# Half-tile loads and per-column value storage in a banded-attention kernel, with up-projection operands in one tile per slice

## The chip, the cores and the metric

The kernel runs on one core of a Trainium2 chip. The core has a matrix engine (TensorE, "PE" in the profile, with its weight loads as "PEld"), VectorE (DVE), ScalarE (ACT), GpSimd (POOL), and SyncE (SP), which in this kernel only issues DMAs; 16 DMA engines carry them. The metric is the device time of one launch in microseconds (us); lower is better.

## The reference

One encoder layer is applied to two sequences, one of 512 tokens (s = 0) and one of 2048 (s = 1), with model width 1024, in float32:

```python
x = layer_norm(x, emb_ln_g, emb_ln_b)
z = x @ w_in                                   # 1024 -> 1952, split in eight parts
o_a = natten(qa, ka, va, na_rpb)               # banded attention on a grid of 64 columns, 4 heads of 64
o_b = fourier_mix(fb)
o_c = mla(cq, ckv, kr, ...)                    # full attention, 4 heads
o_d = spatial_gating(sg, ...)
x = layer_norm(ALPHA * x + concat(o_a, o_b, o_c, o_d) @ w_out)
h = conv3(x @ w_up)                            # 1024 -> 2 * 2816, a convolution of width 3 along tokens
x = layer_norm(ALPHA * x + (gelu(h_gate) * h_val) @ w_down)
```

In `natten` a token in grid row r and column c attends to 8 rows by 16 columns around it. The score has a bias from the table `na_rpb`, taken by the difference of rows and of columns.

## The kernel before

Each float32 product is made of three matmuls: an operand is split into a high part (a rounded copy) and a low part (the rest), and hi·hi, hi·lo and lo·hi are added in PSUM. Intermediate results are kept in DRAM between stages, and every load and store is a DMA that SP issues, in one order. A scheduler sets the order of the instructions on each engine when the program is built, from the order in which the code is written and from buffers that come free; inside the stage `far` the PE order is pinned to that of the code.

The stages that the change touches:

- `near` (first part of phase 1): the first layer norm, and the projections for q, k, v, the gating branch and part of the MLA branch, in five blocks of 512 tokens. `feat` makes q and k with features on partitions, `keyed` makes v with tokens on partitions; both split and store hi and lo. q goes to `zq` as three copies (hi, lo, hi), k to `zk` as two (hi, lo), v to `zv`, indexed by token, head pair, and hi or lo.
- `far` (second part of phase 1): the rest of the projections (600 matmuls of 512 columns, five weight groups by five blocks), in between which the generator `natten` runs the banded attention. Its unit of work is one band of rows, one range of 32 key columns (`CW`, four of them), and one head: 80 units in 10 bands, of 384, 512 or 256 keys. While the matmuls of the projection go on (about six between two units), unit x makes its scores, x-2 is transposed, x-4 is multiplied with the values, x-7 is finished.
- Loads of `natten`: `band` fetches, for two heads, q and k with hi on partitions 0 to 63 and lo on 64 to 127, six units ahead; a second copy of q has the halves exchanged, so that two matmuls give the four products. `window` fetches the values for one range of columns, in chunks of four rows by 32 columns. `table` fetches the bias table, three units ahead, from `R`, where eight rows by 16 columns by n keys are read with overlap; POOL then adds the mask, and DVE adds the table to the scores.
- `ffn_up`: three blocks of at most 900 columns (`FF_BLOCKS`). `operands` transposes x2 (the input) in four slices k of the contraction, builds seven Strassen operands from each (B11, T2, T1, T3, B21, T4, B22) and splits them; `features` then multiplies them, for each of 22 pairs of feature tiles f, with seven weight combinations that `weights` makes in the first block and `weights_again` reloads in the others. Between the features of blocks 2 and 3, `down_ops` prepares the operands of the down-projection, two at a time. An operand is one tile for hi and one for lo, over all four slices; x2 is loaded into two buffers (`xs`), which one slice fills.

Of the kernel before, what the change touches and what calls it, by code (L numbers as in the profile page):

```python
# [15 lines left out]
P = 128  # L16
# [22 lines left out]
HW = 450  # L39
# [65 lines left out]
class Builder:  # L105
# [77 lines left out]
    def build(self):  # L183
        tc, nc, I = self.tc, self.nc, self.I
        with tc.tile_pool(name="cst", bufs=1, reuse_waits="tile") as cst, tc.tile_pool(name="scr", bufs=1, space=bass.MemoryType.DRAM) as scr:
# [24 lines left out]
            self.zq = [[d([3, P, T], f"zq{s}_{j}") for j in range(2)] for s, T in SEQS]  # L210
            self.zk = [[d([2, P, T], f"zk{s}_{j}") for j in range(2)] for s, T in SEQS]
            self.zv = [d([T, 2, 2, P], f"zv{s}") for s, T in SEQS]
# [56 lines left out]
    def phase1(self):  # L269
# [6 lines left out]
        def near(wp, sp, pp):  # L276
# [129 lines left out]
            def feat(b, n, uT=None):  # L406
# [281 lines left out]
    def natten(self, wp, pp):  # L688
# [8 lines left out]
        def band(s, j, i):  # L697
# [3 lines left out]
            for hh in range(2):  # L701
                q = self.t(wp, [P, 2, 4, P], "q", F32R, bufs=4)
                for x in range(2):
                    self.load(q[:, x].bitcast(F32).rearrange("p c q -> p (c q)"),
                              self.zq[s][j][x:x + 2, half[hh], i * 512:(i + 1) * 512])
                self.load(kt[:, hh, :n].bitcast(F32), self.zk[s][j][:, half[hh], r0 * GRID_W:r0 * GRID_W + n])
                qk[s, j, i, hh] = q, kt[:, hh]

        def window(s, j, i, c):
# [3 lines left out]
            z = self.zv[s]  # L713
# [440 lines left out]
    def ffn_up(self):  # L1154
# [7 lines left out]
        with tc.tile_pool(name="xo", bufs=1, reuse_waits="tile") as xo, tc.tile_pool(name="fu", bufs=1, reuse_waits="tile") as sp:  # L1162
# [8 lines left out]
            def operand(name, k, hw, src, lo_eng):  # L1171
                self.split(src, X[name, 0][:, k, :hw], X[name, 1][:, k, :hw], "act", lo_eng)

            def operands(bi):
# [26 lines left out]
                for name in names:  # L1201
                    for i in range(2):
                        X[name, i] = self.t(xo, [P, KH, HW], f"{name}{i}", F32R)
                for k in range(KH):
                    xs = [self.t(self.wr2, [P, 8, P], "xs", bufs=2) for _ in range(2)]
                    for h, (_, pieces) in [(h, x) for h in range(2) for x in halves]:
                        i = 0
                        while i < len(pieces):
                            at, n, c, s, row = pieces[i]
                            x2 = self.x2[s].rearrange("t (h k e) -> t h k e", h=2, k=KH)[:, h, k]  # L1210
                            m = 1
                            while n == P and i + m < len(pieces) and pieces[i + m][1] == P and pieces[i + m][3:] == (s, row + m * P):
                                m += 1
                            if m > 1:
                                self.load(xs[h][:, at:at + m], x2[row:row + m * P].rearrange("(t p) e -> p t e", p=P))
                            else:
                                self.load(xs[h][:n, at], x2[row:row + n])
                            i += m
# [27 lines left out]
                return segs, w, hw  # L1246
# [33 lines left out]
            def product(ps, u, name, hw, first, last):  # L1280
                xh, xl = X[name, 0], X[name, 1]
                mm = nc.tensor.matmul
                for k in range(KH):
                    a, b = u[:, k], u[:, KH + k]
                    mm(ps[:, :hw], a, xh[:, k, :hw], start=first and k == 0, stop=False, skip_group_check=True)  # L1285
                    mm(ps[:, :hw], a, xl[:, k, :hw], start=False, stop=False, skip_group_check=True)  # L1286
                    mm(ps[:, :hw], b, xh[:, k, :hw], start=False, stop=last and k == KH - 1, skip_group_check=True)  # L1287
# [45 lines left out]
            meta = {}  # L1333
# [284 lines left out]
```

## Time and profile before

| | |
|---|---|
| median of 3 runs (lowest, highest) | 3687.84 us (3685.08, 3689.01) |
| the profiled execution: its time, its span | 3691.13 us, 3689.3 us |
| PE, DVE, POOL, ACT busy, share of the span | 86%, 57%, 42%, 38% |
| DMA: bytes, mean rate | 673.10 MB, 182 GB/s |

The profile is of one execution of its own; its sums go against 3691.13 us. A view by windows gives, for a stretch of the span, the busy time of each engine, the granted clock of the PE (1.0 is 2.4 GHz, 0.5 is 1.2 GHz), the mean busy share of the 16 DMA engines and the rate in GB/s. "SPq" is SP's issuing; its time for one issue holds what the issue had to wait for in the DMA queue. `near` ends at 368 us, `natten` at about 1077 us, `ffn_up` begins at about 1931 us.

### The profile page before, as it was taken

Reading aid. Unit: us, or ns where it says so; the run is one execution under the profiler, and the core shown is the slowest. Engines: PE = TensorE matmul, PEld = TensorE weight load, DVE = VectorE, ACT = ScalarE, POOL = GpSimd, SP = SyncE. Lnnn points to the kernel's source line nnn. Section 1 sums busy time; section 2 is a strip of 40 time slices with the busy share of each in tenths; the row PEclk is TensorE's granted clock in tenths of the full one; section 3 lists DMA queues with packets and bytes.
Section 4 is the critical chain, followed back from the end, with each engine's and each line's share of the span. In section 5 each row is a group of like instructions: output and inputs, shape, how many; then the busy total and the mean of one; then the engine's idle time right before and its main releaser. Section 6 shows DMA issues by size and latency. Waiting matters only on the chain.

```text
span 3689.3 us, 47183 instructions
## 1 busy us (share of the span) xinstructions
PE 3182.8 (86%) x16423; PEld 2783.3 (75%) x16423; DVE 2106.2 (57%) x3789; ACT 1417.8 (38%) x2566; POOL 1533.9 (42%) x1267
## 2 busy tenths in 40 slices
PE   6999545434569899999998999999999999999997
PEld 5888334334458788887877999899979998787886
DVE  5352112111226788886456887667555655768778
ACT  4232112111235577665224444444334432325223
POOL 7040001001022467654347887555225421546546
PEclk9999767666789999999999999999999999999999
DMA  8564442324354212113447676799758977657653
GB/s 274 184 223 146 138 127 98 120 88 129 104 165 137 78 29 63 33 31 112 153 148 231 237 244 240 250 338 339 238 186 314 335 269 282 212 201 260 216 190 138
DMA packets 417153, 673.10 MB, mean 182 GB/s; under 512 B 51600, under 2 KB 267760, under 8 KB 413844
## 3 DMA queue, kind: packets, MB, share of 16 engines
q1 hardware_dynamic: 416916, 670.09, 53.0%
q8 instruction: 130, 2.13, 0.2%
q14 instruction: 107, 0.88, 0.1%
HBM read 447.02 MB, written 222.97 MB: 182 GB/s over the span
## 4 chain that ended last, share of the span: by engine, by line
PE 68%; DMA 11%; SPq 10%; DVE 5%; ACT 2%; issue 2%; POOL 2%; DVEq 0%; ACTq 0%; POOLq 0%
SPq L126 9%; PE s L120 9%; PE mm L120 7%; PE s L1286 5%; PE s L1287 5%; PE s L1285 5%; PE t L1480 5%; PE t L1285 4%; PE t L1286 4%; PE t L1287 4%; PE t L120 4%; DMA tbl<-R 3%; PE s L1480 3%; PE o L1480 3%; PE t L980 3%; DMA vt<-zv 2%
## 5 line engine op out<-in xcount | busy, mean ns | idle before, releaser
L144 POOL TENSOR_TENSOR w<-wraw,w 128x512 fp32r<-128x512 f32 x162 | 236.5, 1464 | 315.6 <-ACT w L134 266.1
L730 POOL TENSOR_TENSOR tbl<-tbl,mask 128x384 f32<-128x384 f32 (+2 forms) x60 | 63.2, 1056 | 719.8 <-DMA tbl<-R 716.6
L120 PE MATMUL o<-vt,p 128*128 128x128 f32 x512 | 97.2, 324 | 250.2 <-DMA vt<-zv 138.2
L120 PEld LDWEIGHTS o<-vt,p 128*128 128x128 f32 x512 | 86.2, 234 | 274.1 <-DVE on L775 105.2
L1286 PE MATMUL s<-B,w 128*128 128x450 f32 (+1 forms) x792 | 285.8, 361 | 6.9 <-DVE B L144 6.9
L1285 PE MATMUL s<-B,w 128*128 128x450 f32 (+1 forms) x792 | 285.8, 363 | 0.6 <-ACT B L134 0.6
L1287 PE MATMUL s<-B,w 128*128 128x450 f32 (+1 forms) x792 | 285.5, 360 | 0.0
L1285 PE MATMUL t<-T,w 128*128 128x450 f32 (+1 forms) x792 | 282.5, 361 | 2.9 <-DVE u L1166 1.9
L1287 PE MATMUL t<-T,w 128*128 128x450 f32 (+1 forms) x792 | 284.8, 360 | 0.0
L1286 PE MATMUL t<-T,w 128*128 128x450 f32 (+1 forms) x792 | 284.8, 360 | 0.0
L120 PE MATMUL mm<-a,a 128*128 128x512 f32 x600 | 192.4, 468 | 102.9 <-DMA a<-xd 102.9
L744 DVE CUSTOM_DVE_ANT_0 E<-s,tbl,high 128x384 f32<-128x384 f32 (+2 forms) x80 | 51.4, 642 | 371.7 <-POOL tbl L730 348.5
L120 PEld LDWEIGHTS mm<-a,a 128*128 128x128 f32 x600 | 137.7, 235 | 137.1 <-DMA a<-xd 108.3
L120 PE MATMUL s<-a,Q 96*128 96x512 f32 x816 | 223.0, 405 | 7.7 <-POOL Q L138 3.4
L1293 DVE SCALAR_TENSOR_TENSOR h<-h,convc,h 128x896 f32<-128x896 f32 (+1 forms) x132 | 218.8, 1690 | 0.0
L952 DVE TENSOR_SCALAR_CACHE_REDUCE a<-s,low 128x512 f32<-128x512 f32 x272 | 195.4, 745 | 32.2 <-PE t L980 23.9
L1480 PE MATMUL t<-w,go 128*128 128x512 f32 x696 | 194.6, 399 | 3.8 <-ACT go L134 2.0
L1292 DVE SCALAR_TENSOR_TENSOR h<-h,convc,h 128x896 f32<-128x896 f32 (+1 forms) x132 | 164.6, 1277 | 53.8 <-ACT h L1291 53.8
L1291 ACT ACTIVATE h<-h,convc 128x896 f32<-128x896 f32 (+1 forms) x132 | 138.3, 1095 | 136.3 <-DVE h L1166 135.3
L747 ACT ACTIVATE E<-E,nam 128x384 f32<-128x384 f32 (+2 forms) x80 | 51.0, 637 | 347.3 <-DVE nam L744 347.2
L144 DVE TENSOR_TENSOR a<-t,a 128x512 fp32r<-128x512 f32 x240 | 161.1, 683 | 33.7 <-ACT a L134 32.8
L134 ACT CAST w<-wraw 128x512 fp32r<-128x512 f32 x166 | 102.0, 618 | 188.4 <-PE t L1287 137.9
(326 smaller groups left out, 9039.0 us busy)
## 6 DMA issues: line engine op xcount, KB each, us to landing
w<-wuops SPq DMA_DIRECT2D x220, 512.0 KB
wuops<-w SPq DMA_DIRECT2D x110, 512.0 KB
w<-wdops SPq DMA_DIRECT2D x104, 512.0 KB
wraw<-in_w_up_dram SPq DMA_DIRECT2D x88, 512.0 KB
wdops<-xs SPq DMA_DIRECT2D x74, 512.0 KB
graw<-g SPq DMA_DIRECT2D x100, 256.0 KB
wd<-wdops SPq DMA_DIRECT2D x48, 512.0 KB
a<-xd SPq DMA_DIRECT2D x20, 1024.0 KB
```

Of the source, the lines that this page charges most:

```text
L120: return self.pe(self.nc.tensor.matmul(*a, **k))
L126: self.nc.sync.dma_start(out, in_)
L144: e.tensor_tensor(lo, src, hi.bitcast(F32), op=ALU.subtract)
L952: nc.vector.tensor_scalar(e[:, c * 512:c * 512 + 512], ps, 1.0, self.low, op0=ALU.mult, op1=ALU.max, accum_out=m4[:, c:c + 1])
L980: nc.tensor.transpose(pt[:, k], e[:, kk * P:(kk + 1) * P], self.ident)
L1285: mm(ps[:, :hw], a, xh[:, k, :hw], start=first and k == 0, stop=False, skip_group_check=True)
L1286: mm(ps[:, :hw], a, xl[:, k, :hw], start=False, stop=False, skip_group_check=True)
L1287: mm(ps[:, :hw], b, xh[:, k, :hw], start=False, stop=last and k == KH - 1, skip_group_check=True)
L1291: nc.scalar.activation(c[:, :n], hb[:, 0:n], AF.Identity, bias=cb[:, ft:ft + 1], scale=cw[:, 0, ft:ft + 1])
L1292: nc.vector.scalar_tensor_tensor(c[:, :n], hb[:, 1:n + 1], cw[:, 1, ft:ft + 1], c[:, :n], op0=ALU.mult, op1=ALU.add)
L1293: nc.vector.scalar_tensor_tensor(c[:, :n], hb[:, 2:n + 2], cw[:, 2, ft:ft + 1], c[:, :n], op0=ALU.mult, op1=ALU.add)
L1480: mm = lambda a, b, st, sp_: nc.tensor.matmul(ps, a, b, start=st, stop=sp_, skip_group_check=True)
```

## The change

Four edits:

- `band`: q and k come in one transfer per half (hi or lo) of 64 partitions, in place of one per tile of 128 partitions; so 8 transfers of q and 4 of k per band, before 4 and 2. `zq` has two copies, hi and lo, and no third.
- `keyed` and `window`: the values are kept in four DRAM tensors, one per range of 32 columns, where a chunk of four rows is 128 consecutive rows; a column that lies in two ranges is stored twice. One store of 256 tokens is now 16 of 32 tokens; the loads stay 128, of 128 KB each.
- `ffn_up`: an operand is a tile per slice, with hi and lo in it. The rows of x2 are loaded in a function of their own (`rows_of`), into `xs` for even and `wraw2` for odd slices, two slices ahead; for the next block this begins before the last features of the block. The first weights of a block are made or loaded before its operands.
- `down_ops` is advanced by two and three in turn, and not at the last f of a block.

```diff
-            self.zq = [[d([3, P, T], f"zq{s}_{j}") for j in range(2)] for s, T in SEQS]
+            self.zq = [[d([2, P, T], f"zq{s}_{j}") for j in range(2)] for s, T in SEQS]
-            self.zv = [d([T, 2, 2, P], f"zv{s}") for s, T in SEQS]
+            self.zv = [[d([T // 2, 2, 2 * P], f"zv{s}_{c}") for c in range(4)] for s, T in SEQS]
...
-                for i, a in enumerate((hi, lo, hi) if n[0] == "q" else (hi, lo)):
+                for i, a in enumerate((hi, lo)):
...
-                    r0 = t0 + 2 * t2 * P
-                    self.store(self.zv[s][r0:r0 + 2 * P].rearrange("(t p) j a d -> p t (j a d)", p=P),
-                               z.bitcast(F32).rearrange("p t j a d -> p t (j a d)"))
+                    zz = z.bitcast(F32).rearrange("p t j a d -> p t j (a d)")
+                    for t in range(2):
+                        r0 = (t0 + (2 * t2 + t) * P) // 2
+                        for c in range(4):
+                            for r in range(2):
+                                self.store(self.zv[s][c][r0 + 32 * r:r0 + 32 * r + 32], zz[64 * r + CW[c]:64 * r + CW[c] + 32, t])
...
-                for x in range(2):
-                    self.load(q[:, x].bitcast(F32).rearrange("p c q -> p (c q)"),
-                              self.zq[s][j][x:x + 2, half[hh], i * 512:(i + 1) * 512])
-                self.load(kt[:, hh, :n].bitcast(F32), self.zk[s][j][:, half[hh], r0 * GRID_W:r0 * GRID_W + n])
+                for a in range(2):
+                    for x in range(2):
+                        self.load(q[half[a], x].bitcast(F32).rearrange("p c q -> p (c q)"),
+                                  self.zq[s][j][a ^ x, half[hh], i * 512:(i + 1) * 512])
+                    self.load(kt[half[a], hh, :n].bitcast(F32), self.zk[s][j][a, half[hh], r0 * GRID_W:r0 * GRID_W + n])
...
-                self.load(v[:, k].bitcast(F32), bass.AP(z.tensor, z.offset + ((r0 + 4 * k) * GRID_W + CW[c]) * 512 + j * 256,
-                                                        [[GRID_W * 512, 4], [512, 32], [1, 256]]))
+                self.load(v[:, k].bitcast(F32), self.zv[s][c][(r0 + 4 * k) * 32:(r0 + 4 * k + 4) * 32, j])
...
-                    for i in range(2):
-                        X[name, i] = self.t(xo, [P, KH, HW], f"{name}{i}", F32R)
+                        X[name, k] = self.t(xo, [P, 2, HW], f"{name}{k}", F32R)
...
-                    xs = [self.t(self.wr2, [P, 8, P], "xs", bufs=2) for _ in range(2)]
+                tiles = [self.t(self.wr2, [P, 8, P], ("xs", "wraw2")[k % 2], bufs=2) for _ in range(2)]
...
+            prefetch(0)
+            rows_of(0, 0)
             for bi in range(len(FF_BLOCKS)):
-                meta[bi] = operands(bi)
+                ahead = weights_again(0) if bi else weights(0)
+                if bi == 0:
+                    rows_of(0, 1)
+                operands(bi)
+                last = bi == len(FF_BLOCKS) - 1
                 for f in range(NF):
-                    W = weights_again(f) if bi else weights(f)
-                    if bi:
-                        next(down_ops, None)
-                        next(down_ops, None)
-                    if bi == len(FF_BLOCKS) - 1 and f == NF - 1:
-                        self.down_head()
+                    W = ahead if f == 0 else weights_again(f) if bi else weights(f)
+                    if bi and f < NF - 1:
+                        for _ in range(3 if f % 2 else 2):
+                            next(down_ops, None)
+                    if f == NF - 1:
+                        if last:
+                            self.down_head()
+                        else:
+                            prefetch(bi + 1)
+                            rows_of(bi + 1, 0)
+                            rows_of(bi + 1, 1)
                     features(bi, f, W)
```

SP's queue where `near` gives way to `far`, before: the last stores of k and v, then the first band's q, its mask, tables and values (numbers behind names are those of buffers).

```order
L129 DMA zk_1_26_99<-zs_3252 128x512
L129 DMA zv_28_101<-uv_3306 128x2x512
L129 DMA zv_28_101<-uv_3359 128x2x512
L126 DMA q_3384<-zq_0_21_94 128x1x512 x2
L126 DMA q_3388<-zq_0_21_94 128x1x512 x2
L126 DMA mask_3392<-in_na_mask_dram 128x3x384
L126 DMA tbl_3394<-R_116 128x1x384
```

The same place in the changed kernel, from the second half of the last stores of v on.

```order
L129 DMA zv_0_31_104<-uv_3490 32x512 x2
L129 DMA zv_1_32_105<-uv_3490 32x512 x2
L129 DMA zv_2_33_106<-uv_3490 32x512 x2
L129 DMA zv_3_34_107<-uv_3490 32x512 x2
L126 DMA q_3530<-zq_0_21_94 64x512 x4
L126 DMA q_3537<-zq_0_21_94 64x512 x4
L126 DMA mask_3544<-in_na_mask_dram 128x3x384
L126 DMA tbl_3546<-R_122 128x1x384
```

The two stores of v have become 32 (half of them stand here in part), and the four loads of q eight; the order of mask, tables and values behind them is as it was.

The PE at the change from block 1 to block 2 of `ffn_up`, before (lines L1226 are transposes of x2 for the new block; operands B and T whose last number is below 19000 are still the old block's).

```order
L1226 MATMUL t_19642<-ident_60,xs_19612 128x128 x3
L1226 MATMUL t_19642<-ident_60,xs_19612 128x66
L1285 MATMUL s_19873<-B_4034_19597,w_19845 128x450
L1286 MATMUL s_19873<-B_4035_19598,w_19845 128x450
L1287 MATMUL s_19873<-B_4034_19597,w_19845 128x450
L1226 MATMUL o_19683<-ident_60,xs_19669 128x128 x3
L1226 MATMUL o_19683<-ident_60,xs_19669 128x66
L1226 MATMUL t_19649<-ident_60,xs_19612 128x128 x3
L1226 MATMUL t_19649<-ident_60,xs_19612 128x64
L1285 MATMUL t_19502<-T_3480_16097,w_19479 128x450
```

The same place in the changed kernel.

```order
L1238 MATMUL t_19883<-ident_60,xs_19708 128x128 x3
L1238 MATMUL t_19883<-ident_60,xs_19708 128x66
L1298 MATMUL s_20107<-B_4066_19855,w_19839 128x450
L1299 MATMUL s_20107<-B_4066_19855,w_19839 128x450
L1300 MATMUL s_20107<-B_4066_19855,w_19839 128x450
L1238 MATMUL o_19931<-ident_60,wraw_4046_19717 128x128 x3
L1238 MATMUL o_19931<-ident_60,wraw_4046_19717 128x66
L1238 MATMUL t_19890<-ident_60,xs_19708 128x128 x3
L1238 MATMUL t_19890<-ident_60,xs_19708 128x64
L1298 MATMUL t_19742<-T_3498_16356,w_19699 128x450
```

The sequence is almost the same; the second slice's transposes now read another buffer (`wraw`) than the first slice's.

## Rows read from the trace of the kernel before

**Rows 1.** The page, busy tenths of the PE in 40 slices.
```profile
PE   6999545434569899999998999999999999999997
```

**Rows 2.** Windows: stretch, length, five engines' busy us, PE clock, DMA share, GB/s.
```profile
184.00:368.00 184.00, 183.30 (x1184) 163.70 (x1182) 69.97 (x191) 49.20 (x89) 41.93 (x16) 1.00 0.52 184
368.00:1080.00 712.00, 341.00 (x1532) 279.60 (x1532) 132.40 (x409) 139.21 (x388) 63.20 (x60) 0.70 0.36 117
485.00:500.00 15.00, 0.00 (x0) 0.00 (x0) 0.00 (x0) 0.00 (x0) 0.00 (x0) 0.64 0.13 52
1029.00:1031.00 2.00, 0.06 (x1) 0.09 (x1) 0.56 (x3) 0.03 (x1) 0.72 (x1) 0.50 0.27 92
406.00:408.00 2.00, 0.16 (x1) 0.00 (x0) 0.00 (x0) 0.00 (x0) 0.00 (x0) 0.50 0.47 167
1222.00:1228.00 6.00, 4.46 (x30) 4.32 (x30) 3.41 (x4) 3.31 (x5) 0.00 (x0) 1.00 0.45 142
2400.00:2700.00 300.00, 300.00 (x1462) 275.39 (x1461) 193.66 (x189) 114.67 (x159) 131.44 (x83) 1.00 0.85 297
```

**Rows 3.** Waits, 368 to 1080 us: who waited for whom, us in total, times, longest.
```profile
POOL tbl L730 <- DMA tbl<-R: 716.6, 47, 138.5
```

**Rows 4.** DMA issues of the whole span: out<-in, how many, KB of one.
```profile
vt<-zv SPq DMA_DIRECT2D x128, 128.0 KB
...
q<-zq SPq DMA_DIRECT2D x40, 256.0 KB
...
tbl<-R SPq DMA_DIRECT2D x24, 256.0 KB
...
tbl<-R SPq DMA_DIRECT2D x24, 192.0 KB
...
a<-zk SPq DMA_DIRECT2D x8, 512.0 KB
...
a<-zk SPq DMA_DIRECT2D x8, 384.0 KB
...
a<-zk SPq DMA_DIRECT2D x4, 256.0 KB
```

**Rows 5.** SP's issues by tile: ns of one, least/median/most, first and last start.
```profile
L126 SPq DMA_DIRECT2D q<-zq x40: 509/2652/10237, 381.8 to 1005.4; - x40
...
L129 SPq DMA_DIRECT2D zk<-zs x20: 319/380/1387, 51.9 to 379.6; - x20
...
L126 SPq DMA_DIRECT2D raw<-K x20: 444/450/499, 1222.1 to 1681.2; - x20
```

**Rows 6.** Timeline of the PE (start, us, instruction): scores of successive units.
```profile
421.21 0.60 PE L120 MATMUL s<-a,q 128*128 128x384 f32 x2
421.66 1.55 PE L120 MATMUL mm<-a,a 128*128 128x512 f32 x6
...
423.93 0.60 PE L120 MATMUL s<-a,q 128*128 128x384 f32 x2
...
560.22 0.72 PE L120 MATMUL s<-a,q 128*128 128x512 f32 x2
...
563.51 0.72 PE L120 MATMUL s<-a,q 128*128 128x512 f32 x2
...
992.49 0.49 PE L120 MATMUL s<-a,q 128*128 128x256 f32 x2
...
994.88 0.50 PE L120 MATMUL s<-a,q 128*128 128x256 f32 x2
```

**Rows 7.** Windows where the blocks of `ffn_up` begin.
```profile
1925.00:1965.00 40.00, 24.28 (x117) 18.45 (x116) 30.29 (x58) 19.08 (x37) 28.27 (x21) 0.79 0.73 234
2340.00:2370.00 30.00, 24.68 (x106) 19.14 (x105) 21.37 (x46) 17.40 (x32) 17.70 (x16) 0.83 0.53 161
2740.00:2780.00 40.00, 28.27 (x110) 22.02 (x109) 19.61 (x45) 16.61 (x33) 16.20 (x16) 0.66 0.40 124
```

**Rows 8.** What ended the PE's idle time before the transposes of x2 (us, times).
```profile
DMA xs<-x: 26.0, 16
```

More of the change, by code (lines that the diff above doesn't have):

```diff
@@ L712, in window @@
             v = self.t(wp, [P, 4, 2 * P], "vt", F32R, bufs=4)
-            z = self.zv[s]
             for k in range(nch):
-                self.load(v[:, k].bitcast(F32), bass.AP(z.tensor, z.offset + ((r0 + 4 * k) * GRID_W + CW[c]) * 512 + j * 256,
-                                                        [[GRID_W * 512, 4], [512, 32], [1, 256]]))
+                self.load(v[:, k].bitcast(F32), self.zv[s][c][(r0 + 4 * k) * 32:(r0 + 4 * k + 4) * 32, j])
             V[s, j, i, c] = v
@@ L1171, in operand, with prefetch @@
             def operand(name, k, hw, src, lo_eng):
-                self.split(src, X[name, 0][:, k, :hw], X[name, 1][:, k, :hw], "act", lo_eng)
-            def operands(bi):
+                x = X[name, k]
+                self.split(src, x[:, 0, :hw], x[:, 1, :hw], "act", lo_eng)
+            def prefetch(bi):
                 segs = FF_BLOCKS[bi]
@@ L1200, in operands @@
                     halves.append((zeros, pieces))
-                for name in names:
-                    for i in range(2):
-                        X[name, i] = self.t(xo, [P, KH, HW], f"{name}{i}", F32R)
-                for k in range(KH):
-                    xs = [self.t(self.wr2, [P, 8, P], "xs", bufs=2) for _ in range(2)]
[L1206 to L1218, printed above, removed]
+                staged[bi] = halves, hw, []
@@ new lines, in prefetch, with rows_of @@
+                meta[bi] = segs, w, hw
+            def rows_of(bi, k):
+                halves, hw, xs = staged[bi]
+                tiles = [self.t(self.wr2, [P, 8, P], ("xs", "wraw2")[k % 2], bufs=2) for _ in range(2)]
+                xs.append(tiles)
+                for h, (_, pieces) in [(h, x) for h in range(2) for x in halves]:
+                    i = 0
+                    while i < len(pieces):
+                        at, n, c, s, row = pieces[i]
+                        x2 = self.x2[s].rearrange("t (h k e) -> t h k e", h=2, k=KH)[:, h, k]
+                        m = 1
+                        while n == P and i + m < len(pieces) and pieces[i + m][1] == P and pieces[i + m][3:] == (s, row + m * P):
+                            m += 1
+                        if m > 1:
+                            self.load(tiles[h][:, at:at + m], x2[row:row + m * P].rearrange("(t p) e -> p t e", p=P))
+                        else:
+                            self.load(tiles[h][:n, at], x2[row:row + n])
+                        i += m
@@ L1220, in quarter, with operands @@
+            def operands(bi):
+                halves, hw, staging = staged[bi]
+                for k in range(KH):
+                    xs = staging[k]
+                    for name in names:
+                        X[name, k] = self.t(xo, [P, 2, HW], f"{name}{k}", F32R)
                     def quarter(h, i, tag):
@@ L1245, in operands @@
                     operand("B22", k, hw, b22, "dve")
-                return segs, w, hw
+                    if k + 2 < KH:
+                        rows_of(bi, k + 2)
             def weights(f):
@@ L1280, in product @@
             def product(ps, u, name, hw, first, last):
-                xh, xl = X[name, 0], X[name, 1]
                 mm = nc.tensor.matmul
                 for k in range(KH):
+                    xh, xl = X[name, k][:, 0, :hw], X[name, k][:, 1, :hw]
                     a, b = u[:, k], u[:, KH + k]
-                    mm(ps[:, :hw], a, xh[:, k, :hw], start=first and k == 0, stop=False, skip_group_check=True)
-                    mm(ps[:, :hw], a, xl[:, k, :hw], start=False, stop=False, skip_group_check=True)
-                    mm(ps[:, :hw], b, xh[:, k, :hw], start=False, stop=last and k == KH - 1, skip_group_check=True)
+                    mm(ps[:, :hw], a, xh, start=first and k == 0, stop=False, skip_group_check=True)
+                    mm(ps[:, :hw], a, xl, start=False, stop=False, skip_group_check=True)
+                    mm(ps[:, :hw], b, xh, start=False, stop=last and k == KH - 1, skip_group_check=True)
             def conv(hb, ft, n):
@@ L1331, in features @@
                     col += m + 2
-            meta = {}
+            meta, staged = {}, {}
             down_ops = self.down_ops()
+            prefetch(0)
+            rows_of(0, 0)
             for bi in range(len(FF_BLOCKS)):
-                meta[bi] = operands(bi)
-                for f in range(NF):
-                    W = weights_again(f) if bi else weights(f)
-                    if bi:
-                        next(down_ops, None)
-                        next(down_ops, None)
-                    if bi == len(FF_BLOCKS) - 1 and f == NF - 1:
-                        self.down_head()
+                ahead = weights_again(0) if bi else weights(0)
[3 more added lines that the diff above has]
+                last = bi == len(FF_BLOCKS) - 1
+                for f in range(NF):
+                    W = ahead if f == 0 else weights_again(f) if bi else weights(f)
[5 more added lines that the diff above has]
+                            self.down_head()
+                        else:
+                            prefetch(bi + 1)
+                            rows_of(bi + 1, 0)
+                            rows_of(bi + 1, 1)
                     features(bi, f, W)
```

## The prediction

> **What bounds the kernel now.** I read the PE's slices first. They are full almost everywhere but for one stretch: from slice 5 to slice 12 they stand at 3 to 6 tenths [rows 1]. The windows cut it out: in `far`, 368 to 1080 us, the PE is busy 341 of 712 us, at a mean granted clock of 0.70 [rows 2]. So 371 us are idle there, and part of the rest runs at half speed. The waits say for what: POOL waits 716.6 us for the bias tables [rows 3]. That looks like a matter of the tables, but the DMA engines are busy only 0.36 of the time at 117 GB/s [rows 2], and the same kernel holds 297 GB/s elsewhere (2400 to 2700 us). A queue that is late although its engines are mostly idle has its load on few of them. The window 485 to 500 us shows which transfers do that: SP issues loads of q and k there, no engine computes, and the DMA share is 0.13, which is 2 engines of 16, at 52 GB/s. Where values alone come, it is 0.27 (4 engines) at 92 GB/s; where tables do, 0.47 (8 engines) at 167 GB/s [rows 2].
>
> If these groups lie within each other, the two engines that q and k use must also do their part of all else. The stage moves 117 GB/s x 712 us = 83.3 MB. Of that q is 40 x 256 KB and k 8 x 512, 8 x 384 and 4 x 256 KB, together 18.9 MB; the values are 128 x 128 KB = 16.8 MB; the two larger kinds of table make 11.0 MB [rows 4]; some 36.6 MB are left. At the rates seen: 18.9 / 52 = 363 us, 16.8 / 92 = 182 us, 11.0 / 167 = 66 us, and the rest on 16 engines of 26 GB/s (half of 52), 416 GB/s, 88 us. That is 699 us of 712. So I hold that two DMA engines bound the whole stage, and that the tables are only what waits behind them in the queue.
>
> **What the change does to that stage.** Each q or k transfer becomes two of 64 partitions, with one row per partition on both sides; a value chunk becomes 128 rows on both sides. The nearest row for such a transfer is the load of K in the MLA branch, 64 rows like these: SP issues it in 0.45 us [rows 5], and where four of them and their companions run, the share is 0.45 at 142 GB/s [rows 2]. That is far above 0.13 and 52, with SP's own pace as the likely limit. I take all 16 engines. Then bands take 18.9 / 416 = 45 us, values 40 us, tables 66 us as before, the rest 88 us: 239 us. From the other side, 0.36 x 712 = 256 us is what each engine would do if everything were spread evenly; the tables still use half of the engines, 11.0 MB / 26 GB/s = 423 engine-us or 26 us more there than the mean: 282 us. I take 282, the larger.
>
> In the Trainium skill, "DMA: Bandwidth & Descriptors", section "Why a DMA increments its semaphore by 16 and not by 1", the number of engines of a transfer is the largest up to 16 that divides the size of the outermost dimension on both sides. By it q and k (2 halves) get 2, values (4 rows) 4, tables (8 rows) 8, and the changed loads 16. The trace agrees with 0.13, 0.27 and 0.47; the sum by this rule is the one above.
>
> The PE's floor: units follow each other without a gap in 2.72 us (384 keys), 3.29 us (512) and 2.39 us (256), six projection matmuls included [rows 6]. There are 32, 32 and 16 of them (four, four and two bands of eight): 87 + 105 + 38 = 230 us. The 600 - 480 matmuls outside cost 1.55 / 6 = 0.26 us each [rows 6], 31 us: 261 us at full clock. So PE and DMA come out close to each other, and neither will run free. The highest mean DMA share that a long stretch of this trace holds is 0.85 [rows 2], with the PE full beside it; 282 / 0.85 = 332 us. At the start, 30 more stores of v stand ahead of the first q at about 0.4 us each [rows 5], half of them issued before the last matmuls of `near` end, and the last eight units drain without cover: 20 us for both. Stage: 352 us after 712, **-360 us**. Bounds: 292 us (282 and 10 of drain) and 493 us (the second rival), so -420 to -219.
>
> **The smaller terms.** SP issues 60 more transfers for the bands (60 x 0.45 = 27 us of a queue that now has some 370 to issue in 350 us, below 0.6 us each): hidden by the look-ahead of three to six units, and part of the 0.85. In `near` there are 160 stores of v in place of 10 and 10 fewer of q: 140 x 0.38 to 0.45 us [rows 5] = 53 to 63 us of SP in 368 us, and 2.6 MB more. The PE is busy 183.3 of 184 us in the second half of it [rows 2], since its operands are on the chip; the loads that stand behind these stores are the next block's x, wanted a block later. I take +5 us; 0 if all is covered, 15 if every block start is held by one batch of 32 (12 us) once.
>
> `ffn_up`: in the three stretches where blocks begin, 110 us, the PE does 24.28 x 0.79 + 24.68 x 0.83 + 28.27 x 0.66 = 58 us of work at full clock [rows 7]; 52 us are lost. Of that 26.0 us are the PE waiting for the rows of x2 [rows 8], because `xs` holds one slice. With two slices ahead this wait can go. What is late next is the building of operands, four slices on DVE, ACT and POOL: DVE is busy 30.29 of the first 40 us [rows 7]. The tile per slice by itself gives little: a slice's old operand is free less than one product earlier (12 of the 84 matmuls of an f, some 2.4 us), and the PE's order at the boundary is nearly as before. I take -20 us; 0 if operands simply become the wait, -40 if the clock stays up too, and a loss of up to 10 if buffers shared with the weights hold something up. `down_ops` at 2.5 per f for 30 f in place of 2 for 37: an operation moves 0.67 MB (a store of 512 KB, and a seventh of two loads of as much), and an f lasts 17 us (1462 matmuls in 300 us, 84 per f), so half an operation more is 19 GB/s on 297 [rows 2]: share 0.90, no cost; up to 10 us if the weights come late in the f with three.
>
> **Sum.** 3691.1 (the profiled execution) - 360 - 20 + 5 = 3316 us; the median of the shown runs lies 3.3 us below the profiled one: **3313 us**.
>
> **Rivals.**
> 1. Look-ahead and clock take much of it back. For it: tables are fetched three units ahead, some 9 us, and a band's burst (2 MB and a mask, and projection operands of 1 MB each) goes through the same queues; one issue of q took up to 10.2 us [rows 5]; after each gap the PE runs at half clock. If the mean clock stays at 0.70, the PE alone needs 261 / 0.70 = 373 us, and a wait of 10 us in each of ten bands gives 473; with the 20 us, 493 us. Total 3691 - 219 - 15 = 3457. Against it: bursts shorten most of all.
> 2. The stage runs on its floor, 292 us, and the block starts give 30: 3691 - 420 - 30 = 3241. For it: where no transfer is late, units already follow each other without a gap [rows 6]; against: DMA and PE would both have to be over 0.9 busy.
> 3. Slower: the halves bring nothing, because two transfers to 64 partitions take as long together as the one took, and SP only has more to issue. It decides if a half runs at 52 GB/s or less. Then the stage stays at 712 us, plus 60 x 0.45 = 27 us, plus 12 us of stores ahead of the first band: 3691 + 39 = 3730. Against it: 142 GB/s for K's 64 rows [rows 2].
>
> The skill's same page, in "Rules for kernel authors", advises against two transfers to disjoint partition halves, since both use all engines already. By that rule the third rival holds; the window with 0.13 says that here the one transfer does not use all engines.
>
> **Chances.** The forecast 0.66 (its own range 3250 to 3390), rival 1 0.18, rival 2 0.11, rival 3 0.05. The range 3220 to 3455 holds the forecast, nearly all of rival 2 and half of rival 1. What this measurement can tell from no change is about 0.2%, 7 us. All but rival 3 are faster: 0.95; its 0.05 I split into 0.04 slower and 0.01 within, where losses and small gains would cancel.
>
> **What would show it.** In the changed profile: no stretch with a share of 0.13 in `far`; the first score within 20 us of the end of `near`; the stage's DMA share near 0.75, its clock above 0.9; POOL's wait for tables below 300 us, since POOL, not a bound, always waits for the next one; the PE's gaps before transposes of x2 without the rows' DMA. The forecast is wrong if q still comes at 52 GB/s, if the stage is over 450 us, or if the tables, still on eight engines, have become what all units wait for.

## The result, and the profile after

The changed kernel takes 3313.2 us (median of 3 runs, 3308.36 to 3321.07), the kernel before 3687.84: ratio 0.8988, 95% interval 0.8959 to 0.9017. The prediction was 3313 us. The profiled execution took 3308.36 us (span 3306.6), 382.7 us of span less than that of before.

The PE by slices, and its granted clock, after. The stretch of 3 to 6 tenths [rows 1] is gone; slices 5 to 9 (counted from 1, as there) stand at 8, and the clock there at 8 to 9 tenths.

```profile
PE   6799888889899999999999999999899999999997
...
PEclk9899998989899999999999999999899999999999
```

Windows after: the second half of `near`, `far` from end to end, and three parts of it (columns as in [rows 2]).

```profile
193.00:377.00 184.00, 182.52 (x1180) 162.96 (x1179) 71.41 (x196) 51.13 (x93) 41.92 (x16) 1.00 0.64 210
...
376.80:708.30 331.50, 275.79 (x1520) 235.38 (x1519) 127.66 (x401) 136.71 (x383) 63.50 (x60) 0.90 0.83 240
...
400.00:500.00 100.00, 85.75 (x484) 73.79 (x485) 43.66 (x129) 45.35 (x119) 25.32 (x22) 0.91 0.86 254
500.00:600.00 100.00, 85.08 (x481) 73.23 (x480) 42.55 (x129) 44.60 (x123) 20.84 (x18) 0.90 0.91 251
600.00:700.00 100.00, 82.39 (x454) 70.27 (x452) 36.88 (x132) 41.36 (x127) 17.34 (x20) 0.90 0.84 247
```

The bytes are nearly those of before (331.5 us x 240 GB/s = 80 MB, before 83), and the busy time is near that of before: 0.83 x 331.5 = 275 us of each DMA engine, before 0.36 x 712 = 256. What changed is that all 16 share it; only the tables are still read by eight. The PE's idle time in the stage fell from 371 to 56 us. Its waits in `far`, first before, then after (engine, line, what it waited for: us, times, longest):

```profile
PE o L120 <- DMA vt<-zv: 138.2, 45, 30.6
PE mm L120 <- DMA a<-xd: 102.9, 11, 41.1
PE o L120 <- DVE on L775: 95.0, 14, 32.0
```

```profile
PE o L120 <- DVE on L777: 20.5, 9, 4.7
PE mm L120 <- DMA a<-xd: 12.6, 5, 5.5
PE s L120 <- DMA q<-zq: 7.7, 2, 7.4
PE t L123 <- ACT E L749: 7.5, 3, 5.4
PE o L120 <- DMA vt<-zv: 7.2, 4, 5.6
```

The operands `xd` of the projection have the same 16-engine shape before and after; no edit touches them. They cost 103 us before and 12.6 after; with q and k alone back on two engines (the first experiment below) it is 85.8 us again. So they were late because of what stood ahead of them in the queue. To cut the span into stages, the first and last starts of three groups on the PE, before:

```profile
L120 PE MATMUL mm<-wtok,xTl x320: 279/290/443, 50.8 to 367.8; 128*128 128x256 f32 x80, 128*128 128x288 f32 x80
L120 PE MATMUL o<-vt,p x512: 219/277/477, 423.0 to 1077.0; 128*128 128x128 f32 x171
L1226 PE MATMUL o<-ident,xs x96: 217/273/476, 1931.0 to 2771.5; 128*128 128x128 f32 x68, 64*128 64x64 f32 x8, 1*128 1x1 f32 x8, 65*128 65x65 f32 x4
```

and after:

```profile
L120 PE MATMUL mm<-wtok,xTl x320: 277/290/446, 52.4 to 376.5; 128*128 128x256 f32 x80, 128*128 128x288 f32 x80
L120 PE MATMUL o<-vt,p x512: 220/276/475, 411.2 to 708.0; 128*128 128x128 f32 x171
L1238 PE MATMUL o<-ident,xs x48: 217/272/478, 1563.0 to 2384.2; 128*128 128x128 f32 x34, 64*128 64x64 f32 x4, 1*128 1x1 f32 x4, 65*128 65x65 f32 x2
```

With the start of the last up-projection matmul (3104.7 and 2722.2 us) this gives the ledger:

| part | before, us | after, us | change | predicted |
|---|---|---|---|---|
| to the end of `near` | 367.8 | 376.5 | +8.7 | +5 |
| `far`, to the last value matmul | 709.2 | 331.5 | -377.7 | -360 |
| from there to `ffn_up` | 854.0 | 855.0 | +1.0 | 0 |
| `ffn_up` | 1173.7 | 1159.2 | -14.5 | -20 |
| the rest | 584.6 | 584.4 | -0.2 | 0 |

SP's issues after (ns of one, least/median/most, first and last start); q before was 2652 in the median and up to 10237 [rows 5]:

```profile
L126 SPq DMA_DIRECT2D q<-zq x80: 444/587/1087, 388.7 to 663.6; - x80
```

So it was the backlog of the queue, not the issuing, that took 2.7 us. The median alone is no safe sign of such a queue: with q and k back on two engines it is only 655 ns, and the backlog shows in the longest issue.

```profile
L126 SPq DMA_DIRECT2D q<-zq x40: 493/655/9776, 407.8 to 913.7; - x40
```

### The profile page after: what moved, and what is told of

Its sections match the earlier page's. It is cut to its first block, busy times and chain, and to the rows that moved or that the text cites. A ratio compares the mean times of both kernels' runs of the same rounds, so it can differ in the third digit from the quotient of the medians.

```text
span 3306.6 us, 47401 instructions
## 1 busy us (share of the span) xinstructions
PE 3118.1 (94%) x16423; PEld 2737.1 (83%) x16423; DVE 2112.2 (64%) x3789; ACT 1417.7 (43%) x2566; POOL 1537.0 (46%) x1267
## 4 chain that ended last, share of the span: by engine, by line
PE 41%; DVE 4%; DMA 2%; issue 1%; POOL 1%; ACT 1%; SPq 0%; DVEq 0%; POOLq 0%; ACTq 0%
PE s L1299 6%; PE s L1298 6%; PE s L1300 6%; PE t L1504 5%; PE t L1298 4%; PE t L1299 4%; PE t L1300 4%; PE s L1504 3%; PE o L1504 3%; DMA graw<-g 1%; DVE x L1371 1%; DVE go L144 1%; POOL w L144 1%; DMA wraw<-x 0%; DVE x L1487 0%
## 5 line engine op out<-in xcount | busy, mean ns | idle before, releaser
L732 POOL TENSOR_TENSOR tbl<-tbl,mask 128x384 f32<-128x384 f32 (+2 forms) x60 | 63.5, 1060 | 344.8 <-DMA tbl<-R 332.0
L1306 DVE SCALAR_TENSOR_TENSOR h<-h,convc,h 128x896 f32<-128x896 f32 (+1 forms) x132 | 219.6, 1694 | 0.0
L1305 DVE SCALAR_TENSOR_TENSOR h<-h,convc,h 128x896 f32<-128x896 f32 (+1 forms) x132 | 171.5, 1330 | 53.4 <-ACT h L1304 53.4
L120 PE MATMUL mm<-a,a 128*128 128x512 f32 x600 | 167.8, 422 | 12.6 <-DMA a<-xd 12.6
L120 PEld LDWEIGHTS s<-a,Q 96*128 96x128 f32 x816 | 145.2, 192 | 33.4 <-DVE a L954 4.5
L134 ACT CAST a<-t 128x512 fp32r<-128x512 f32 x240 | 134.1, 585 | 79.2 <-PE t L982 76.5
L982 PE MATMUL t<-ident,a 128*128 128x128 f32 x1088 | 156.2, 275 | 9.6 <-DVE a L144 5.5
L1504 PEld LDWEIGHTS t<-w,go 128*128 128x128 f32 x696 | 130.5, 188 | 40.0 <-ACT go L134 4.4
L134 ACT CAST go<-gs 128x256 fp32r<-128x256 f32 x200 | 78.0, 405 | 195.4 <-PE t L1504 64.7
```

What stands on the lines that cost most here:

```text
L120: return self.pe(self.nc.tensor.matmul(*a, **k))
L134: nc.scalar.copy(out, src)
L982: nc.tensor.transpose(pt[:, k], e[:, kk * P:(kk + 1) * P], self.ident)
L1305: nc.vector.scalar_tensor_tensor(c[:, :n], hb[:, 1:n + 1], cw[:, 1, ft:ft + 1], c[:, :n], op0=ALU.mult, op1=ALU.add)
L1306: nc.vector.scalar_tensor_tensor(c[:, :n], hb[:, 2:n + 2], cw[:, 2, ft:ft + 1], c[:, :n], op0=ALU.mult, op1=ALU.add)
L1504: mm = lambda a, b, st, sp_: nc.tensor.matmul(ps, a, b, start=st, stop=sp_, skip_group_check=True)
```

## The experiments

Times are medians; the kernel before, run beside each of them, took 3687.6 to 3689.7 us, so they can be read against 3313.2 directly.

**Bands undone.** Ratio to before 0.9674 (0.9659 to 0.9688), 3567.8 us.

```diff
-                for a in range(2):
-                    for x in range(2): self.load(q[half[a], x]..., self.zq[s][j][a ^ x, half[hh], ...])
-                    self.load(kt[half[a], hh, :n]..., self.zk[s][j][a, half[hh], ...])
+                for x in range(2): self.load(q[:, x]..., self.zq[s][j][x:x + 2, half[hh], ...])
+                self.load(kt[:, hh, :n]..., self.zk[s][j][:, half[hh], ...])
```

> The changed kernel with the loads of q and k (and the three copies of q) as in the kernel before; values, operands and tables stay changed. Theory A (how many of the 16 DMA engines carry a transfer is set by its outermost dimension, and the fullest engines bound the stage): two engines carry q and k again, 18.9 MB at 52 GB/s = 363 us, and their part of values 40, tables 66 and the rest 88: 557 us for a stage that now takes 331.5 us. far 560 to 600 us, DMA share there near 0.45, whole time 3540 to 3580 us. Theory B (the gain comes from the values' layout, or from look-ahead that any relief gives back): less than 60 us lost, below 3370 us.

`far` of this kernel as a window:

```profile
376.50:974.00 597.50, 304.24 (x1520) 256.10 (x1520) 132.78 (x408) 142.74 (x386) 63.28 (x60) 0.73 0.44 141
```

597.5 us, at a share of 0.44. The sum for two engines, 557 us, is 0.93 of it; in the kernel before it was 699 of 712. The values' layout alone, with q and k on two engines, brings the other 112 us of the stage, no more.

**Values undone.** Ratio 0.9280 (0.9268 to 0.9293), 3422.5 us.

```diff
-                self.load(v[:, k]..., self.zv[s][c][(r0 + 4 * k) * 32:(r0 + 4 * k + 4) * 32, j])
+                self.load(v[:, k]..., bass.AP(z.tensor, ..., [[GRID_W * 512, 4], [512, 32], [1, 256]]))   # and one store per 256 tokens
```

> The changed kernel with the values stored and loaded as before; q and k still come as halves. Theory A: the four engines that values use carry 45 (q, k) + 182 (values) + 66 (tables) + 88 (rest) = 381 us; far 390 to 440 us in place of 331.5, and near gives back its 8.7 us, since 10 stores of v stand there again in place of 160: whole time 3360 to 3410 us. Theory B (values were hidden behind q and k and bound nothing): far within 15 us of 331.5, whole time 3290 to 3315 us. If near does not come back to 368 us, its 8.7 us were not the stores of v.

```profile
370.20:817.60 447.40, 317.32 (x1519) 261.29 (x1519) 126.99 (x401) 134.48 (x383) 63.29 (x60) 0.81 0.58 175
```

The direction of theory A, but 12 us beyond its range: four engines' 381 us make 447, 0.85 and not 0.93 or more of the stage. The last matmul of `near` starts at 369.9 us, so 6.6 of its 8.7 us were the stores of v; in the kernel with `ffn_up` changed alone it starts at 370.1 with the old stores, so the other 2 us are scatter. From both runs: the bands are worth 255 us, the values 109, each with the other already mended.

**`ffn_up` undone, and `ffn_up` alone.** Two kernels: the changed one with the old `ffn_up` (3325.3 us, ratio 0.9017, 0.9004 to 0.9029), and the one before with the new one (3676.7 us, ratio 0.9967, 0.9954 to 0.9979).

```diff
-                        X[name, k] = self.t(xo, [P, 2, HW], f"{name}{k}", F32R)   # and rows_of, first weights, down_ops
+                    for i in range(2): X[name, i] = self.t(xo, [P, KH, HW], f"{name}{i}", F32R)
```

> The changed kernel with ffn_up, its operands and the pace of down_ops as before: the attention part alone. If the two parts add up, the whole time is 14.6 us above that of the changed kernel, by the markers in the two traces: ratio to the kernel before 0.902 to 0.904, near 3327 us. Rival: the 14.6 us are what the slices of x2 wait for in a queue that the attention left late, so that ffn_up is quick by itself: then no loss, ratio 0.898 to 0.900.

> The kernel before with the edit of ffn_up alone (tile per slice, rows of x2 loaded ahead, first weights ahead of the operands, down_ops at 2.5). If it adds up: 14.6 us less, 3673 us, ratio 0.996, the PE's wait for the rows of x2 going from 26.0 us to 22 or less. Rival: no difference within 0.2%.

12 us each way: the parts add up, and `ffn_up` doesn't depend on what the attention does to the queue. In the second kernel the PE's own wait for the rows falls from 19.0 to 8.8 us.

**Rows not ahead.** 3328.4 us, ratio 0.9021 (0.9008 to 0.9035).

```diff
-                tiles = [self.t(self.wr2, [P, 8, P], ("xs", "wraw2")[k % 2], bufs=2) for _ in range(2)]
+                tiles = [self.t(self.wr2, [P, 8, P], "xs", bufs=2) for _ in range(2)]   # rows_of(bi, k) inside the loop over k
```

> The changed kernel with the rows of x2 loaded into the two xs buffers alone, one slice at a time inside the loop over slices, as before; the tile per slice, the first weights ahead of the operands and the pace of down_ops stay changed. If the rows' early loading is what makes ffn_up shorter (the prediction's step), all of its 14.6 us are lost: about 3325 us. If the tile per slice or the weights' earlier place do it, less than 5 us are lost, since the PE still waited 22.1 us for rows in the changed kernel: 3310 to 3318 us.

All of the gain is lost (15 us), so the early rows make it. The PE's waits over the block starts, changed kernel:

```profile
PE t L1238 <- DMA wraw<-x: 7.1, 7, 2.5
...
PE t L1238 <- DMA xs<-x: 2.7, 1, 2.7
...
PE o L1238 <- DMA wraw<-x: 0.6, 1, 0.6
```

and without the early rows:

```profile
PE t L1239 <- DMA xs<-x: 16.0, 6, 5.8
PE s L1298 <- DVE B L144: 7.0, 2, 6.4
PE o L1239 <- DMA xs<-x: 3.2, 5, 1.6
```

10.4 us for the rows against 19.2; and the 7.0 us for the operand B, which is built from them, go with it. `ffn_up` takes 1174.1 us in this run, as long as before the change (1173.7). So the tile per slice, the first weights ahead and the new pace of `down_ops`, which all stayed in, bring nothing that shows; none of them was taken out by itself. The second theory rested on a misreading: the 22.1 us that it named count the PE and its weight loads together, whose waits overlap.

**Stores of v merged.** 3305.3 us, ratio 0.8961 (0.8947 to 0.8974).

```diff
-                                self.store(self.zv[s][c][r0 + 32 * r:r0 + 32 * r + 32], zz[64 * r + CW[c]:64 * r + CW[c] + 32, t])
+                            self.store(dst[r], zz[64 * r + CW[c]:64 * r + CW[c] + 32])   # both t: dst "(t r p) j e -> r p t j e"
```

> The changed kernel with the 16 stores of 32 tokens per 256 tokens of v made 8 of 2 x 32 (the same bytes, 80 issues in place of 160 in near). If the end of near was late (376.8 us for 368.1 before, and the first score 16 us later) because SP issues so many stores, half of both goes: 4 to 10 us less, 3300 to 3309 us. Rival: the bytes, not the issues, hold up the loads: no change within 0.15%, 3308 to 3318 us.

SP where `near` gives way to `far`, changed kernel (start, us, what, how many):

```profile
372.54 16.01 SPq L129 DMA_DIRECT2D zv<-uv  x32
388.65 4.93 SPq L126 DMA_DIRECT2D q<-zq  x8
```

with merged stores:

```profile
365.83 9.29 SPq L129 DMA_DIRECT2D zv<-uv  x16
375.22 5.15 SPq L126 DMA_DIRECT2D q<-zq  x8
```

The same bytes in half the issues: the last matmul of `near` starts at 369.8 us, 6.7 us earlier, and the first q is issued 13.4 us earlier. `far` stays about as long (333.4 us in this run); the medians differ by 8.

**Tables over 16 engines.** 3295.6 us, ratio 0.8928 (0.8912 to 0.8943).

```diff
-            self.load(t[:, :n], bass.AP(self.R.tensor, self.R.offset + a0, [[32, 8], [1, 16], [1, n]]))
+            self.load(t[:, :n], bass.AP(self.R.tensor, self.R.offset + a0, [[1, 16], [32, 8], [1, n]]))   # q, mask, result in that order
```

> The changed kernel with the 128 queries of a unit in another order (16 columns outermost, 8 rows inside), so that a table is read as 16 x 8 x n in place of 8 x 16 x n; q is stored, the mask built and the result put back in that order. Bytes, issues and instructions are the same. Theory A (outermost dimension sets the engines, fullest engine bounds far): the tables spread over 16 engines, the fullest one has 256 us in place of 282, far 331.5 to about 305, whole time 3280 to 3295 us. Rival C (the PE with its half-speed stretches and the queue's order now bound the stage): far within 6 us, whole time 3305 to 3320 us.

```profile
378.80:690.10 311.30, 268.80 (x1519) 231.46 (x1519) 127.90 (x401) 140.38 (x383) 63.29 (x60) 0.92 0.91 255
```

20 us of `far`, where 26 was the price of the unevenness: theory A, at a slightly smaller size (the whole time is 0.6 us above its range).

**One transfer per tile, 128 rows.** 3269.3 us, ratio 0.8855 (0.8837 to 0.8873).

```diff
-            self.zq = [[d([2, P, T], f"zq{s}_{j}") for j in range(2)] for s, T in SEQS]
+            self.zq = [[d([2, 3 * 64, T], f"zq{s}_{j}") for j in range(2)] for s, T in SEQS]   # per head: hi, lo, hi
...
+                for x in range(2): self.load(q[:, x]..., self.zq[s][j][hh, 64 * x:64 * x + P, ...])
```

> The changed kernel, but q and k lie in DRAM per head with the halves behind each other, so that one transfer fills 128 partitions from 128 rows: 2 + 1 transfers per head of a band as in the kernel before (60 fewer issues in far), yet 128 rows outermost; q has its third copy again, and near stores q and k in 64-row pieces (60 more stores). Theory A (the outermost dimension matters, not the halving): far within 15 us of 331.5, whole time 3295 to 3325 us. Theory B (two smaller transfers side by side are what brings the gain): far falls back towards the 597 us that it took with whole tiles of outermost dimension 2, whole time above 3400 us.

```profile
372.80:666.30 293.50, 261.55 (x1519) 226.85 (x1519) 127.66 (x401) 141.21 (x383) 63.67 (x60) 0.94 0.86 270
```

Neither range: 44 us faster than the changed kernel, in the profiled executions 38.0 of them in `far` and 4.0 in `near`, whose stores of q and k this edit changes too. The outermost dimension is what matters, and the halving itself is a loss. The next three runs ask why; they keep the stores of this one.

**Halves again, contiguous and interleaved; empty issues.** Three edits of the kernel with one transfer per tile:

```diff
-                    self.load(q[:, x]..., self.zq[s][j][hh, 64 * x:64 * x + P, ...])
+                    self.load(q[h, x]..., self.zq[s][j][hh, 64 * x:64 * x + P, ...][h])   # h = 0:64, 64:128, or 0::2, 1::2; k alike
...
+                for y in range(3): self.load(d[half[y % 2]], self.zk[s][j][hh, half[y % 2], i * 512:i * 512 + 4])   # third run
```

> The kernel of the earlier run with one 128-row transfer per tile of q and k (3269 us), each transfer cut again into two of 64 rows, for partitions 0 to 63 and 64 to 127: the loads of the changed kernel from another DRAM layout. If it is the cutting that costs 44 us, by the number of issues or by the 64 partitions, the time is back at 3300 to 3320 us. If it was the DRAM layout (the rows of hi and lo close to each other), it stays at 3265 to 3280 us.

> The same, but each of the two transfers of 64 rows takes every other row and every other partition of the tile (0, 2, 4, ... and 1, 3, 5, ...): as many issues, rows and bytes, from the same DRAM layout. Theory D (a transfer into one half of the partitions is slower, since packets of 4 KB took longer in the changed kernel): 3265 to 3285 us, the issue of a load of q near 0.34 us. Theory E (the number of issues, or 64 rows on 16 engines, costs the time): 3300 to 3320 us like contiguous halves, the issue near 0.59 us.

> The kernel with one 128-row transfer per tile of q and k (3269 us), and 60 more loads in the bands, three per head, each of 64 partitions by 16 bytes into a tile that nobody reads: the issues of the interleaved halves (3293 us) without a change in how the bytes travel. If the number of issues is the 24 us between those two: 3288 to 3298 us. If it is the transfer of 64 rows by itself (its issue of 0.59 us against 0.34, its rows on the engines): 3265 to 3280 us.

Measured: contiguous halves 3313.8 us (ratio 0.8984, 0.8971 to 0.8998), interleaved 3293.1 (0.8931, 0.8916 to 0.8945), empty issues 3299.6 (0.8949, 0.8934 to 0.8964). Contiguous halves bring back the whole loss from another layout in DRAM, so it is the cutting that costs. (The two kernels with contiguous halves agree as a whole, not by stages: in this run `near` ends 6.1 us earlier than in the changed kernel and `far` is 13.1 us longer. So that the layout in DRAM costs nothing in `far` is not shown.) Of the 44 us some 20 go with the 64 neighbouring partitions, and the other 24 stay with a second transfer of any kind. The interleaved halves lie outside both of their ranges: between theories D and E, each has about half, while the issue of a load of q (0.59 us in the median) is E's. The empty issues came out 1.6 us above their range, and outside the rival's. `far` with contiguous, then with interleaved halves:

```profile
370.70:715.30 344.60, 280.63 (x1519) 238.75 (x1518) 127.69 (x401) 136.28 (x383) 63.48 (x60) 0.89 0.85 230
```

```profile
371.40:690.10 318.70, 271.93 (x1519) 232.68 (x1518) 127.53 (x401) 136.50 (x383) 63.56 (x60) 0.92 0.81 249
```

Share times length is the mean busy time of an engine for the same 79 MB: 293 us with contiguous halves, 258 interleaved, 252 with one transfer. It is 275 and 287 in the changed kernel and in the one with merged stores, which have contiguous halves too, so the size of the effect scatters, but not its sign. The single packets in the traces say the same: the 768 packets of 4 KB in `far`, which are rows of k, took 286 ns in the mean in the changed kernel, 291 with contiguous halves again, 200 interleaved and 174 with one transfer. So transfers into 64 neighbouring partitions make the packets themselves longer. (Interleaved, the rows in DRAM are every other one as well; the runs don't part the two sides.) The other half is not bytes: 60 loads of 1 KB each cost 30 us. They stand ahead of the next tables. SP at the second band of the changed kernel, from the last table ahead of the band's loads to the first behind them, then POOL, which takes that one:

```profile
422.20 0.59 SPq L126 DMA_DIRECT2D tbl<-R  x1
422.89 3.70 SPq L126 DMA_DIRECT2D vt<-zv  x4
426.63 1.13 SPq L126 DMA_DIRECT2D q<-zq  x2
427.86 0.53 SPq L126 DMA_DIRECT2D a<-zk  x1
...
435.89 0.59 SPq L126 DMA_DIRECT2D a<-zk  x1
436.58 1.00 SPq L126 DMA_DIRECT2D a<-xd  x2
437.68 0.62 SPq L126 DMA_DIRECT2D tbl<-R  x1
...
448.98 1.26 POOL L732 TENSOR_TENSOR tbl<-tbl,mask 128x512 f32<-128x512 f32 x1 [18.49 <-DMA tbl<-R]
```

With one transfer per tile:

```profile
413.59 0.59 SPq L126 DMA_DIRECT2D tbl<-R  x1
414.85 0.32 SPq L126 DMA_DIRECT2D q<-zq  x1
416.52 1.74 SPq L126 DMA_DIRECT2D vt<-zv  x4
418.31 0.43 SPq L126 DMA_DIRECT2D q<-zq  x1
418.84 0.38 SPq L126 DMA_DIRECT2D a<-zk  x1
420.43 0.84 SPq L126 DMA_DIRECT2D q<-zq  x2
421.31 0.43 SPq L126 DMA_DIRECT2D a<-zk  x1
421.84 1.27 SPq L126 DMA_DIRECT2D tbl<-R  x2
```

From table to table it is 15.5 us in the first and 8.3 in the second, with four loads of values in both (and two of `xd` in the first). Tables are fetched three units ahead, some 9 us; in the first case POOL sits 18.49 us without one. With empty issues the two tables on either side of this band's loads are again 15.5 us apart (418.27 and 433.75 us), and POOL sits 17.17 us without one.

How long DVE then waits for POOL's table in `far`, first in the changed kernel, then with one transfer:

```profile
DVE E L746 <- POOL tbl L732: 80.3, 34, 13.4
```

```profile
DVE E L746 <- POOL tbl L732: 12.7, 11, 2.9
```

It is 90.2 us with contiguous halves again, 62.5 interleaved and 51.8 with empty issues. With merged stores, where the loads are those of the changed kernel, it is 100.7, so differences of 20 us between these say nothing; that to 12.7 does.

**All three together** (one transfer per tile, tables over 16 engines, merged stores): 3232.3 us (3230.22 to 3239.69), ratio 0.8768 (0.8755 to 0.8781), the fastest version.

> The three gains together: one 128-row transfer per tile of q and k, tables read over 16 engines, stores of v merged to 8 per 256 tokens. The gains over the changed kernel one by one were 44, 18 and 8 us. If they add up: 3243 us. In far they can't: by the floor of the PE (261 us of matmuls and about 20 for start and drain) far can go from 293.5 to 281 at the least, so 3250 us is the more likely, 3240 to 3262 us; no gain over 3269 us would say that the PE's order, not the DMA, is the bound already.

```profile
364.40:631.40 267.00, 252.41 (x1519) 220.74 (x1518) 127.83 (x401) 141.71 (x383) 63.34 (x60) 0.97 0.94 296
```

The gains add up and 11 us more come on top, so the expected range was missed from below. Its floor of 281 us for `far` was wrong: `far` takes 267.0. The PE is busy 0.95 of it, the DMA engines 0.94: both bounds at once, which the prediction had thought unlikely. Why the three together give more than their sum was not taken apart.

## Why the prediction was right, step by step

- **Two engines bound the stage.** Held. Counted from the single packets of the trace (it does not name their engines), at least two were under way in 707 of the 709 us of `far` before, and only two or three in 321 of them. Undoing the bands gave 597.5 us for a sum of 557. For four engines the same sum came out 15% short (381 for 447), and not because they paused: at least four packets were under way in 438 of the 447 us. So the rates, each read where one kind of load ran alone, were too high for loads that run together; which kind slows down by how much was not taken apart.
- **The changed loads use all 16.** Held. In steps of 15 us from 378 to 693 us the DMA share lies between 0.55 (the first) and full; nothing like 0.13 [rows 2] is left while there are loads. (Then they are over: 0.10 in the last 15 us.) By the Trainium skill ("DMA: Bandwidth & Descriptors", "Why a DMA increments its semaphore by 16 and not by 1"), the count of engines follows the outermost dimension; three runs here agree, with 2 and 4 undone and 8 made 16 (3567.8, 3422.5 and 3295.6 us).
- **The stage: 282 us of DMA at a share of 0.85, and 20 for start and drain.** 352 predicted, 331.5 measured; two terms were wrong, and they cancelled in part. The busiest eight engines had more to do than 282 us: the half-tile transfers raised the mean from 256 to 275, which with the 26 for the tables makes 301, and at least eight packets were under way in 306 of the 331.5 us. And there was less beside it: 25 us, where the prediction had 50 (the share of 0.85) and 20 for start and drain. Of the 25, the first 16 us and the last 18 hold 11. The 0.85 is no ceiling: the last kernel holds 0.94 through `far`. The first score came 16.5 us after `near`, as predicted within 20, and the projection's matmuls ran in that time (8.88 us of 16.2).
- **`near` +5.** 8.7 measured, inside the 0 to 15. The stores of v make it, and not by their bytes: merged, with the same bytes in 80 issues fewer, 6.7 us of it are gone. That the count of issues alone decides is not shown: the kernels with one transfer per tile, with halves again and with empty issues have all 160 of these stores and 60 more of q and k, and their last matmul of `near` starts at 370.4 to 372.5 us, not at 376.5. Nor is it the last batch of 32: most of the time is lost between 92 and 184 us, where the PE is busy 79.40 us and was busy 84.39. Why was not taken apart.
- **`ffn_up` -20.** 14.5 measured, inside its bounds, with its cause as predicted. The mis-sized term is the wait for rows. Of the 26.0 us of [rows 8], which add up the PE and its weight loads, the PE's own part was 19.0, and it is nearly halved (10.4), not gone; what is left is mostly for `wraw`, the buffer of the odd slices. The PE's 6.9 us for an operand B behind the rows, which the prediction had not priced by themselves, went as well.
- **The sum.** 3313 for 3313.2 us is nearer than its terms are, and that is luck: `far` gave 17.7 us more than forecast, `near` and `ffn_up` together 9.2 less, and the profiled execution lies 4.8 us below its median, where that of before lies 3.3 above.
- **Rival 1** was true in kind: bursts delay the tables (POOL waits ten times 7 to 22 us for one after the first), and the PE idles 56 us in `far` at a clock of 0.90. It had priced that at ten times 10 us and a clock of 0.70, and half the idle time was there.
- **The signs.** Of six that were named, two came: no stretch at 0.13, and the first score in time. The share is 0.83, not near 0.75; the clock 0.90, not above; the PE still waits for the rows of x2; and POOL waits 332.0 us for tables, not below 300 (270.6 with one transfer). The last was a poor sign: 116.7 us of it are the wait for the first table, which begins in `near`.
- **Rival 3**, that halves bring nothing but issues, was wrong as a whole and right in its part: a half costs what the prediction booked at nothing ("hidden by the look-ahead"). The 60 issues were not hidden; they stood in front of tables that were due within some 9 us. In "Rules for kernel authors" of "DMA: Bandwidth & Descriptors" the Trainium skill says to use one transfer of 128 partitions; with all rows outermost that is 44 us faster here than two halves, while one transfer with the halves outermost was 255 us slower than two. The rule holds, on condition that the one transfer has many rows in its outermost dimension.

## What to carry to other kernels

Where a queue is late and the DMA share is low, read the share in a short window in which one kind of load runs alone: here 0.13, 0.27 and 0.47 were 2, 4 and 8 engines, and the remedy is to lay the data out in DRAM so that the rows are the outermost dimension of one whole transfer, not to cut the transfer. Price a burst by what stands behind it in the queue: an issue is hidden only if the first thing due behind the burst is due later than the burst is long. A mean share times the length of a stage, compared between versions, tells longer packets from idle engines.

## What was not expected

An issue of 64 rows takes SP longer than one of 128: at least 444 ns for 64 rows of q here, 445 for 64 rows of 16 bytes, 315 for 128 rows of q with one transfer per tile. It is the shape, not the bytes, and not simply the number of rows: the stores of 32 rows of v took 302 at least. The loads of 64 rows by 16 bytes, all of the third run:

```profile
L126 SPq DMA_DIRECT2D dum<-zk x60: 445/503/1482, 384.4 to 637.7; - x60
```

Why 64 neighbouring partitions make packets longer and every other partition doesn't was not taken apart further.
